# A seven-product matrix kernel on one core: two weight sums queued at the front, and one more stage split a third time

## The chip, the cores and the metric

The kernel runs on one core of one Trainium2 chip. The metric is the device time of an execution in microseconds (us), from the host's view of the device; a profiled execution also has a span, from its first to its last instruction. A core has TensorE (PE, matrix products into PSUM banks), VectorE (DVE, elementwise work), ScalarE (ACT), GpSimd (POOL) and SyncE (SP); in this kernel the last two only start transfers, apart from a small mask at the beginning. Every engine works through its own instructions in order and waits on semaphores of the others.

## The reference

A mixture of eight experts with soft routing: softmax over the experts for each token, and the weighted sum of the experts' matrix products.

```
x (16, 512, 512)   router_logits (16, 512, 8)   expert_weights (8, 512, 2048)
probs = softmax(router_logits)
output = sum over e of probs[:, :, e:e+1] * matmul(x, expert_weights[e])    # (16, 512, 2048) float32
```

## The kernel before

**One large product.** With Z = the tokens' x, scaled by each expert's probability and laid side by side (8192 x 4096), the output is Z times all weights stacked (4096 x 2048). Operands are f16, sums f32. The left operand is made on VectorE, by `times`: x transposed (`xT`) times the probabilities broadcast over partitions (`pT`).

**Three levels of seven products.** A 2 x 2 block product can be made of seven products in place of eight, at the price of sums on both sides (Strassen's way). The kernel does it on three levels.

- Outer level: P1 to P7, on halves of the tokens (pairs of 256 rows, `2q` and `2q + 1`, q from 0 to 15), of the experts and of the columns. `right[r]` holds P_r's weights, `Left` its left operand, `Product` one P_r of one q: 256 rows, depth 2048, 1024 columns.
- Inner level: each of those is seven inner products, run in the order `STEPS = (1, 5, 6, 2, 7, 3, 4)`. Each is 8 matmuls of 128 x 512. Weights 5, 6, 7 and 4 are sums of the four raw blocks, made by `inner_sums` on VectorE: four subtractions over 128 x 4096 (tile `w`). Sum 6 needs sum 5, sum 4 needs sum 6, and sum 7 is written over the block that sum 5 reads. On the left, `queue_s2` makes `d` (for inner product 6) and `queue_i` makes `i` (a `z` made of `z` and `d`, for inner products 7 and 3).
- Third level, in some stages: inner products 1 and 5 of a stage's two products are split into seven again, `by_thirds`: 14 small products of 4 matmuls over 256 columns in place of 4 whole ones. `Thirds.make` makes four left sums for it (128 x 1024), `third_sums` the weights; two of the seven results are added by VectorE in 128 x 256 pieces, on each of the two columns.

**Stages and slots.** A stage is two products, and its inner products alternate: 14 slots, the first product in even slots, the second in odd ones. `run` goes through the stages: P1 in stages 0 to 6 (`ND` = 7 is the first stage of P2), then P2, then P5 and P6, then stage `k7`, which holds P6's last product (6,15) in even slots and P7's first (7,0) in odd ones, then 15 stages of P4 and P7, then P3. A stage by thirds has its inner products 1 and 5 in slots 0 to 3. Before the change, stages 1 to 5 of P1 are by thirds, and stage 6, its last pair, is not. In stage `k7`, inner product 7 of (7,0) is slot 9, and its inner product 4 slot 13.

**What sets VectorE's order.** The program order of VectorE and ScalarE is fixed as the program is written. A planner keeps two clocks, of PE and of VectorE, by costs written in the code (`SLOT` 1.73 for an inner product, 2.29 for a weight sum, 1.22 for a left operand). Work for VectorE is put into `queue` by `later` (at its end, or in front with `first=True`); after each inner product, `slack` takes tasks from the front while VectorE's clock is behind PE's by more than `LAG`. `need` takes all tasks up to one that PE's next step uses, and `flush` is what it uses for that. Evacuations of banks (`post`) are not queued: they are written out where they fall. Hooks put in by `at(stage, slot, ...)` run before the slot's inner product: `sums_at` queues weight sums in this way. After a stage's first slot, `queue_lefts` queues all left operands of the next stage.

P7's four sums are queued by the `sums_at` of line 1086: 5 and 6 in stage `k7 - 1`, 7 in slot 3 of stage `k7`, 4 in its slot 7. P2's are queued in stage 6 (lines 957 to 960).

Of the kernel before, what the change touches and what calls it, by code (L numbers as in the profile page):

```python
# [31 lines left out]
def kernel(  # L32
# [73 lines left out]
    def tt(o, a, b, op):  # L106
        dve(nc.vector.tensor_tensor(out=o, in0=a, in1=b, op=op))  # L107
# [15 lines left out]
    def bank():  # L123
        return psum.tile([P, NB], f32, name="ps", tag="ps")

    def bank2():
        return psum.tile([P, NB], f32, name="pt", tag="pt", bufs=2)
# [6 lines left out]
    def new_w():  # L134
        return wpool.tile([P, K8, NB], f16, name="w", tag="w")

    def new_u():
        return zpool.tile([P, K8, HQ], f16, name="u", tag="u", bufs=1)

    def new_z():  # L140
        return zpool.tile([P, K8, HQ], f16, name="z", tag="z")
# [25 lines left out]
    def inner_sums(b, t7=None):  # L167

        w = {1: b[0, 0], 2: b[1, 0], 3: b[1, 1], 7: t7 or b[0, 1]}

        def step(p, x, y):
            if p not in w:
                w[p] = new_w()
            tt(w[p], x, y, SUB)
        return w, {5: lambda: step(5, b[0, 1], b[0, 0]), 6: lambda: step(6, b[1, 1], w[5]),
                   4: lambda: step(4, b[1, 0], w[6]), 7: lambda: step(7, b[1, 1], b[0, 1])}
# [145 lines left out]
    for n in range(2):  # L322
        ps = [bank2() if n == 0 and j < 2 else bank() for j in range(4)]
        for e in range(HE):
# [4 lines left out]
            if n == 0 and e == 2:  # L329
# [3 lines left out]
                w, sums = inner_sums(b11, new_w())  # L333
# [36 lines left out]
    def flush(task):  # L370
        while task is not None and not task.done:
            queue.popleft().run()

    def need(task):
        if task is not None and not task.done:
            flush(task)
            clock["pe"] = max(clock["pe"], clock["dve"])

    def later(cost, make, first=False):
        t = Task(cost, make)  # L380
        (queue.appendleft if first else queue.append)(t)
        return t
# [58 lines left out]
    def times(z, k, xb, pb):  # L441
        tt(z.rearrange("p (e c) t -> p e c t", e=2), xb.t.unsqueeze(1).to_broadcast([P, 2, C, HQ]),
           pb.t[:, ds(2 * k, 2)].unsqueeze(2).to_broadcast([P, 2, C, HQ]), MUL)

    class Left:
# [6 lines left out]
        def make(self, k):  # L452
            if self.of is not None:
                need(self.of.task[k])
            t = self.t[k] = new_z()
            times(t, k, self.xb, self.pb)
            if self.less is not None:
                u = new_u()
                times(u, k, *self.less)
                tt(t, t, u, SUB)  # L460
            if self.of is not None:
                tt(t, self.of.t[k], t, SUB)
            if self.kept is not None:
                tt(t, t, self.kept.t[:, ds(k * K8, K8), :], SUB)
# [80 lines left out]
    class Right:  # L545
# [6 lines left out]
            self.w, sums = inner_sums(b)  # L552
            return sums

        def queue_sum(self, sums, p):
            self.task[p] = later(2.29, sums[p])

        def op(self, p):
            need(self.task.get(p))
# [65 lines left out]
    ND = 7  # L625
# [28 lines left out]
    def at(stage, slot, make):  # L654
        hooks.setdefault((stage, slot), []).append(make)

    def add(*products):
        stages.append(products)
        return len(stages) - 1


    right = {r: Right() for r in (2, 5, 6, 7, 4, 3)}
# [33 lines left out]
    def product(r, q, **how):  # L696
        left, loads = left_of(r, q)
        lefts[r, q] = left
        p = None
        if r == 1:  # L700
            def sink(tn, o):
                pool(kept_rows(q)(tn), o)
            p = Product(right[1], left, sink)
        elif r == 2:
            if q >= ON_BASE:
                bases[2, q] = Base(kept_rows(q))
            p = Product(right[2], left, to_out(q, 0, 0), bases.get((2, q)))
        elif r == 5:
            bases[6, q] = m1 = Base(kept_rows(q))
            m1.task = {}  # L710

            p = Product(right[5], left, to_out(q, 1, 0))
        elif r == 6:
            m1 = bases[6, q]

            def base(tn):
                need(m1.task[tn])
                return m1.t[tn]
            p = Product(right[6], left, to_out(q, 0, 1), base)
        elif r == 7:  # L720
            base = bases[7, q] = Base(lambda tn: out_rows(q, 0, 1, tn))
            p = Product(right[7], left, to_out(q, 1, 1), base)
        elif r == 4:
            p = Product(right[4], left, to_out(q, 1, 0, accum_op=ADD), products[7, q].o.__getitem__)
        else:
            p = Product(right[3], left, to_out(q, 0, 1, accum_op=ADD), **how)
        p.loads = loads
        products[r, q] = p
        return p
# [137 lines left out]
    k7 = add(some, product(7, 0))  # L867
# [74 lines left out]
    b21, t2 = {}, {}  # L942
# [4 lines left out]
    for kn, where in zip(((0, 0), (0, 1), (1, 1), (1, 0)), ((1, 8), (3, 2), (5, 0), (5, 9))):  # L947
        at(*where, lambda kn=kn: cast21(kn))

    def sums_at(stage, slot, r, of, ps):  # L950
        def go():
            if right[r].w is None:
                right[r].sums = right[r].build(of)
            for p in ps:
                right[r].queue_sum(right[r].sums, p)
        at(stage, slot, go)
    sums_at(ND - 1, 3, 2, b21, (5,))
    sums_at(ND - 1, 5, 2, b21, (6,))
    sums_at(ND - 1, 7, 2, b21, (7,))
    sums_at(ND - 1, 12, 2, b21, (4,))  # L960
    ODD = 0, 1
    for i, (kn, e) in enumerate((kn, e) for kn in (ODD, (0, 0), (1, 1), (1, 0)) for e in range(2)):
        stage = ND + i - 2 if kn != ODD else 2 + 2 * i
        wedge_at(stage, 2, kn, e, (stage + 1, 0))

    def fetch_at_w(stage, slot, of, what, kn):
        at(stage, slot, lambda: of.__setitem__(kn, fetch_w(what, kn)))
# [101 lines left out]
    def turnover(stage, place, r, raw, every=3):  # L1069

        right[r].w = {}

        def fetch(p):
            if p in RAW:
                right[r].w[p] = fetch_w(raw, RAW[p])
            else:
                right[r].w[p] = fetch_w((r, p), (0, 0))
        if every == 3:
            at(stage - 1, 9, lambda: fetch(1))
        for i, p in enumerate(STEPS[every == 3:]):  # L1080
            at(*slots_after(stage, place + 1, every * i), lambda p=p: fetch(p))
    t3 = {}
    for slot, kn in zip((0, 2, 4, 6), ORDER):
        fetch_at_w(k7 - 1, slot, t3, "t3", kn)
    for stage, slot, p in ((k7 - 1, 10, 5), (k7 - 1, 13, 6), (k7, 3, 7), (k7, 7, 4)):
        sums_at(stage, slot, 7, t3, (p,))
    turnover(k7, 0, 4, "t4")
    turnover(k3 - 1, 1, 3, "b22", 2)

# [68 lines left out]
            post(p)  # L1158
    finish.step, finish.post = step_at_end, post_at_end

    for stage in range(1, ND - 1):
        thirds[stage] = Thirds(*(p.left for p in stages[stage]), third)
    for stage in range(ND + 1, last2):
        thirds[stage] = Thirds(*(p.left for p in stages[stage]), third2)
# [44 lines left out]
```

## Time and profile before

| | |
|---|---|
| median of 3 runs | 1374.52 us (1374.25 to 1374.65) |
| profiled execution | 1374.57 us |
| its span | 1372.5 us |
| mean granted clock of TensorE | 0.996 |
| VectorE busy | 1130.7 us, 82% of the span |
| ScalarE busy | 258.8 us, 19% |

How to read it: "PE" rows are matmuls; they are pipelined, so the duration of one (379 ns) is longer than the step from one to the next. "PEld" is the loading of the left operand, which overlaps. All elementwise instructions of VectorE have line 107, that of the helper `tt`, and all matmuls line 130, so they are told apart by tiles: `w` a weight block, `z` a left operand, `d` the left operand of inner product 6, `u` a part of a left operand of two pairs, `xT` and `pT` what it is made of, `ps` and `pt` PSUM banks, `h` results and other half-size tiles. In a timeline, a bracket behind a row gives the idle time before it and what ended it. A group of windows has, for each, its length and the busy time of PE, PEld, DVE, ACT and POOL with the number of instructions, then the granted clock, the share of the DMA engines and GB/s.

### The profile page before, as it was taken

Reading aid. Unit: us, or ns where it says so; the run is one execution under the profiler, and the core shown is the slowest. Engines: PE = TensorE matmul, PEld = TensorE weight load, DVE = VectorE, ACT = ScalarE, POOL = GpSimd, SP = SyncE. Lnnn points to the kernel's source line nnn. Section 1 sums busy time; section 2 is a strip of 40 time slices with the busy share of each in tenths; the row PEclk is TensorE's granted clock in tenths of the full one; section 3 lists DMA queues with packets and bytes.
Section 4 is the critical chain, followed back from the end, with each engine's and each line's share of the span. In section 5 each row is a group of like instructions: output and inputs, shape, how many; then the busy total and the mean of one; then the engine's idle time right before and its main releaser. Section 6 shows DMA issues by size and latency. Waiting matters only on the chain.

```text
span 1372.5 us, 18682 instructions
## 1 busy us (share of the span) xinstructions
PE 1355.9 (99%) x6822; PEld 665.0 (48%) x6822; DVE 1130.7 (82%) x1365; ACT 258.8 (19%) x517; POOL 435.8 (32%) x667
## 2 busy tenths in 40 slices
PE   9999999999999999999999889999999999999998
PEld 4555545565544444444444334444444444556554
DVE  7876677878899888887878987888989888898884
ACT  3233313242211111111111100000000000233331
POOL 3223323332222323223221113344443434233341
PEclk9999999999999999999999989999999999999999
DMA  9999979898999999999987977999999999999997
GB/s 183 245 218 266 246 222 227 256 243 248 255 333 290 281 311 288 281 262 298 299 265 266 345 257 192 229 255 264 255 265 234 270 259 308 336 304 247 207 159 136
DMA packets 190683, 353.55 MB, mean 258 GB/s; under 512 B 52992, under 2 KB 81920, under 8 KB 185856
## 3 DMA queue, kind: packets, MB, share of 16 engines
q0 software_dynamic: 89824, 189.31, 59.1%
q1 hardware_dynamic: 97456, 139.86, 33.8%
q10 hardware_dynamic: 3312, 23.20, 4.4%
q8 instruction: 53, 0.87, 0.3%
q14 instruction: 38, 0.31, 0.1%
HBM read 208.44 MB, written 180.55 MB: 283 GB/s over the span
## 4 chain that ended last, share of the span: by engine, by line
PE 98%; DVE 1%; DMA 0%; issue 0%; POOL 0%; ACT 0%; DVEq 0%; POOLq 0%
PE ps L130 74%; PE pt L130 24%; DVE z L107 1%; DMA w<-in_x_dram 0%; DVE h L107 0%; DVE u L107 0%; DVE w L107 0%; DVE d L107 0%; DVE z L255 0%; POOL w L121 0%; ACT h L1155 0%; DVE lg L295 0%; DVEq L107 0%; POOLq L1193 0%
## 5 line engine op out<-in xcount | busy, mean ns | idle before, releaser
L130 PE MATMUL ps<-w,z 128*128 128x512 f16 (+1 forms) x3768 | 822.1, 375 | 10.9 <-DVE w L107 10.9
L130 PEld LDWEIGHTS <-z 128*128 128x128 f16 x5272 | 516.0, 98 | 590.5 <-issue 13.7
L121 POOL DMA_DIRECT2D out_dram<-h x380 | 256.0, 706 | 698.8 <-ACT h L614 274.2
L130 PE MATMUL pt<-w,z 128*128 128x512 f16 (+1 forms) x1504 | 317.9, 359 | 0.0
L107 DVE TENSOR_TENSOR z<-xT,pT 128x2048 f16<-128x2048 f16 x220 | 265.9, 1216 | 3.5 <-PE pt L130 2.6
L107 DVE TENSOR_TENSOR h<-ps,h 128x512 f32<-128x512 f32 x248 | 168.9, 687 | 95.4 <-PE ps L130 75.3
L130 PE MATMUL ps<-w,d 128*128 128x512 f16 x880 | 199.1, 379 | 0.0
L601 ACT COPY h<-ps 128x512 f32<-128x512 f32 x118 | 69.2, 586 | 420.2 <-PE ps L130 394.3
L130 PEld LDWEIGHTS <-d 128*128 128x128 f16 x880 | 86.0, 98 | 100.1
L107 DVE TENSOR_TENSOR z<-z,d 128x2048 f16<-128x2048 f16 x110 | 131.8, 1216 | 0.0
L107 DVE TENSOR_TENSOR h<-pt,h 128x512 f32<-128x512 f32 x125 | 85.2, 687 | 50.9 <-PE pt L130 49.2
L107 DVE TENSOR_TENSOR w<-w 128x1024 f16<-128x1024 f16 (+2 forms) x105 | 112.3, 1086 | 1.9 <-PE ps L130 1.0
L614 ACT COPY h<-ps 128x512 f32<-128x512 f32 x50 | 29.3, 586 | 402.5 <-PE ps L130 364.6
L107 DVE TENSOR_TENSOR d<-z 128x1024 f16<-128x1024 f16 x110 | 74.6, 684 | 4.5 <-PE ps L130 3.4
L107 DVE TENSOR_TENSOR ps<-ps,h 128x512 f32<-128x512 f32 (+1 forms) x88 | 51.0, 582 | 26.7 <-PE ps L130 23.3
L597 ACT COPY h<-ps 128x512 f32<-128x512 f32 x95 | 52.6, 605 | 70.7 <-PE ps L130 70.7
L121 POOL DMA_DIRECT2D kept<-h x56 | 30.7, 548 | 93.9 <-ACT h L601 53.8
L121 POOL DMA_DIRECT2D out_dram<-kept x56 | 56.4, 1042 | 12.2 <-DMA out_dram<-h 6.3
L593 ACT COPY ps<-ps 128x512 f32<-128x512 f32 x59 | 33.6, 570 | 121.0 <-PE ps L130 65.3
L107 DVE TENSOR_TENSOR ps<-pt,h 128x256 f32<-128x256 f32 x36 | 15.5, 432 | 38.7 <-PE pt L130 26.6
L107 DVE TENSOR_TENSOR h<-h 128x512 f32<-128x512 f32 (+2 forms) x69 | 45.1, 675 | 1.1 <-DMA h<-kept 0.9
L107 DVE TENSOR_TENSOR z<-z,u 128x2048 f16<-128x2048 f16 x36 | 44.1, 1225 | 1.2
(73 smaller groups left out, 543.9 us busy)
## 6 DMA issues: line engine op xcount, KB each, us to landing
out_dram<-h POOLq DMA_DIRECT2D x380, 256.0 KB, 7.3
pT<-p_dram SPq DMA_DIRECT2D x126, 256.0 KB, 7.2
w<-wd ACTq DMA_DIRECT2D x22, 1024.0 KB, 9.5
xT<-x SPq DMA_DIRECT2D x80, 256.0 KB, 7.5
h<-kept SPq DMA_DIRECT2D x72, 256.0 KB, 8.2
h<-out_dram SPq DMA_DIRECT2D x68, 256.0 KB, 6.0
w<-in_expert_weights_dram POOLq DMA_DIRECT2D x33, 512.0 KB, 10.2
kept<-h POOLq DMA_DIRECT2D x56, 256.0 KB, 5.2
```

Of the source, the lines that this page charges most:

```text
L107: dve(nc.vector.tensor_tensor(out=o, in0=a, in1=b, op=op))
L121: note(nc.gpsimd.dma_start(out=o, in_=i, **how))
L130: note(nc.tensor.matmul(ps, z, w, start=start, stop=stop, skip_group_check=True))
L593: act(nc.scalar.copy(self.banks["b"], x))
L597: act(nc.scalar.copy(o[tn], q if p == 5 else x))
L601: act(nc.scalar.copy(o[TN[p]], b if p == 2 else x))
L614: act(nc.scalar.copy(o[tn], b))
```

## The change

P7's sums 7 and 4 are queued one slot later than before (slots 4 and 8 of stage `k7`), but at the front of the queue. As a sum at the front can come ahead of a sum that it depends on, `queue_sum` takes that one first. Stage 6, P1's last, is run by thirds as well, and three of P2's four sums, which are queued in stage 6, are queued two slots later each.

```diff
-        def queue_sum(self, sums, p):
-            self.task[p] = later(2.29, sums[p])
+        def queue_sum(self, sums, p, first=False):
+            def make():
+                flush(self.task.get({6: 5, 7: 5, 4: 6}.get(p)))
+                sums[p]()
+            self.task[p] = later(2.29, make, first)
...
-    def sums_at(stage, slot, r, of, ps):
+    def sums_at(stage, slot, r, of, ps, first=False):
...
-                right[r].queue_sum(right[r].sums, p)
+                right[r].queue_sum(right[r].sums, p, first)
...
-    sums_at(ND - 1, 3, 2, b21, (5,))
-    sums_at(ND - 1, 5, 2, b21, (6,))
-    sums_at(ND - 1, 7, 2, b21, (7,))
+    sums_at(ND - 1, 5, 2, b21, (5,))
+    sums_at(ND - 1, 7, 2, b21, (6,))
+    sums_at(ND - 1, 9, 2, b21, (7,))
...
-    for stage, slot, p in ((k7 - 1, 10, 5), (k7 - 1, 13, 6), (k7, 3, 7), (k7, 7, 4)):
-        sums_at(stage, slot, 7, t3, (p,))
+    for stage, slot, p in ((k7 - 1, 10, 5), (k7 - 1, 13, 6), (k7, 4, 7), (k7, 8, 4)):
+        sums_at(stage, slot, 7, t3, (p,), p in (7, 4))
...
-    for stage in range(1, ND - 1):
+    for stage in range(1, ND):
         thirds[stage] = Thirds(*(p.left for p in stages[stage]), third)
```

## The prediction

> **What bounds the kernel now.** I read the page first. One engine sets the time, TensorE (PE): 1355.9 us busy in a span of 1372.5. The run that was profiled took 1374.57 us, 2.07 more than its span, and the median of the runs before is 1374.52; I make the sum against 1374.57 and leave the 0.05 alone.
>
> ```profile
> span 1372.5 us, 18682 instructions
> PE 1355.9 (99%) x6822; PEld 665.0 (48%) x6822; DVE 1130.7 (82%) x1365; ACT 258.8 (19%) x517; POOL 435.8 (32%) x667
> ```
>
> Time can therefore come off in two ways: fewer matmul columns, or less PE idle time. The second view is the list of waits for PE alone, and it has one entry of weight.
>
> ```profile
> PE ps L130 <- DVE w L107: 10.9, 1, 10.9
> PE every L89 <- DVE h L86: 1.3, 1, 1.3
> ```
>
> One wait of 10.9 us on a weight sum (tile `w`) made by VectorE (DVE). Third view: the timeline of PE around it. Columns are start, duration, engine, line, operation, tiles, count.
>
> ```profile
> 775.74 3.62 PE L130 MATMUL ps<-w,d 128*128 128x512 f16 x16
> 779.20 5.34 PE L130 MATMUL ps<-w,z 128*128 128x512 f16 x24
> 795.46 3.57 PE L130 MATMUL ps<-w,z 128*128 128x512 f16 x8 [10.92 <-DVE w L107]
> 798.82 3.79 PE L130 MATMUL pt<-w,z 128*128 128x512 f16 x16
> 802.46 3.83 PE L130 MATMUL ps<-w,z 128*128 128x512 f16 x17
> ```
>
> An inner product is 8 matmuls and takes one slot. 775.74 to 779.20 is 16 matmuls, so a slot is 1.73 us. The `d` operands mark inner product 6, slots 4 and 5 of a stage; this is stage k7, where P6's last product (6,15) and P7's first (7,0) alternate. Slots 6, 7 and 8 run from 779.20, so slot 8 starts at 782.65 and slot 9 could start at 784.38. It is inner product 7 of (7,0), it needs P7's weight sum 7, and it starts at 795.46: 11.08 us late (the view counts 10.92, from the end of the last matmul). What does DVE do meanwhile? Its timeline:
>
> ```profile
> 774.08 2.28 DVE L107 TENSOR_TENSOR w<-w 128x4096 f16<-128x4096 f16 x1
> 776.27 1.28 DVE L107 TENSOR_TENSOR h<-pt,h 128x512 f32<-128x512 f32 x2
> 777.67 0.69 DVE L107 TENSOR_TENSOR h<-ps,h 128x512 f32<-128x512 f32 x1
> 778.28 0.68 DVE L107 TENSOR_TENSOR h<-h 128x512 f32<-128x512 f32 x1
> 778.88 1.22 DVE L107 TENSOR_TENSOR z<-z,d 128x2048 f16<-128x2048 f16 x1
> 780.01 0.68 DVE L107 TENSOR_TENSOR h<-ps,h 128x512 f32<-128x512 f32 x1
> 780.61 1.22 DVE L107 TENSOR_TENSOR z<-z,d 128x2048 f16<-128x2048 f16 x1
> 781.75 1.22 DVE L107 TENSOR_TENSOR z<-xT,pT 128x2048 f16<-128x2048 f16 x1
> ...
> 784.74 0.68 DVE L107 TENSOR_TENSOR h<-ps,h 128x512 f32<-128x512 f32 x1
> ...
> 789.60 1.22 DVE L107 TENSOR_TENSOR z<-xT,pT 128x2048 f16<-128x2048 f16 x1
> ...
> 793.12 4.49 DVE L107 TENSOR_TENSOR w<-w 128x4096 f16<-128x4096 f16 x2
> 799.07 0.69 DVE L107 TENSOR_TENSOR h<-ps,h 128x512 f32<-128x512 f32 x1 [1.46 <-PE ps L130]
> ```
>
> DVE is never idle from 774.08 to 797.6. The two sums that PE needs in slots 9 and 13 stand last, at 793.12, behind the left operands of the *next* stage (781.75 to 793.12). So this is an order problem: work that is due later stands first. After it PE waits for nothing, while DVE waits 1.46 us for PE at 799.07.
>
> The wait has a second price. Windows of the clock (the column behind POOL is the granted clock):
>
> ```profile
> 787.50:788.50 1.00, 0.00 (x0) 0.00 (x0) 0.97 (x2) 0.00 (x0) 0.00 (x0) 1.00 0.99 397
> 788.50:789.50 1.00, 0.00 (x0) 0.00 (x0) 0.97 (x2) 0.00 (x0) 0.00 (x0) 0.72 1.04 412
> 797.40:798.40 1.00, 1.00 (x4) 0.30 (x3) 0.21 (x1) 0.00 (x0) 0.00 (x0) 0.50 1.01 422
> 798.40:799.40 1.00, 1.00 (x4) 0.40 (x3) 0.33 (x1) 0.00 (x0) 0.00 (x0) 0.61 1.00 420
> ```
>
> At 0.72 the second window spent (0.72 - 0.50)/0.50 = 0.44 us at full clock: the clock halves at 788.94, 4.4 us after PE stopped at 784.54. By the last window it is back at 799.18, 3.7 us after PE resumed. From 795.46 to 802.46 PE did 24 matmuls in 7.00 us, where three slots take 5.18: 1.82 us lost.
>
> **Part 1: the two sums go to the front.** In the built program, VectorE's order from the row at 777.67 on becomes: evacuation of 6.6 (inner product 6 of (6,15)), *sum 7*, evacuation of 7.6, `h<-h`, first `z<-z,d` (operand i of (6,15)), *sum 4*, evacuation of 6.7, second `z<-z,d` (operand i of (7,0)), then the next stage's operands among later evacuations. Nothing is added; two instructions of 4096 columns pass nine or more others. Both are wanted by PE in this stage, but so are the two `z<-z,d`, in slots 8 and 9, and those are now later. I walk it through on the clock of before. Steps from start to start: a sum 2.21 (4.49 for two, less the last one's 2.28), an `h` 0.60 (780.01 to 780.61), a `z` 1.13 (778.88 to 780.01), its result 1.22 after its start, and some 0.04 to reach PE. An evacuation can start 0.36 after its slot (784.74 against 784.38).
>
> - Sum 7: 778.28 to 780.49. PE wants it at 784.38; it is 3.9 us early and this wait is gone.
> - Evacuation of 7.6 to 781.09, `h<-h` to 781.69.
> - i of (6,15): starts 781.69, ready 782.95. Slot 8 wants it at 782.65: **a new wait of 0.30**. Slot 8 ends at 784.68.
> - Sum 4: 782.82 to 785.03. It is wanted only in slot 13, and it stands ahead of i of (7,0).
> - Evacuation of 6.7: can start 784.68 + 0.36 = 785.04, to 785.64.
> - i of (7,0): starts 785.64, ready 786.90. Slot 9 could have started at 784.68: **a new wait of 2.22**.
>
> Slot 9 starts at 786.90 in place of 795.46. New waits together are 2.52 us, against 11.08. The price of these waits is bounded by 0 below (DVE done in time) and 11.08 above (the whole backlog still ahead); I take 2.52 because each of its steps has its own row.
>
> With 0.30 and 2.22 us, both under the 4.4 that passed before the clock halved, I take the 1.82 as saved too. [...]
>
> What is late next: DVE enters stage k7+1 with a backlog, where it was idle in before. Going on with the same steps: PE begins that stage at 786.90 + 5 x 1.73 = 795.5. The first left operand of (7,1) (a `z`, `u`, `z` group takes 3.52: 789.60 to 793.12) is ready at 794.9 and wanted in slot 1, at 797.3. The evacuation of 7.1 by 7.1's own base, which PE's slot 5 has to wait for (same bank), ends at 803.0; slot 5 starts at 804.2. That is the tightest place, with 1.1 us to spare. Later stages have room:
>
> ```profile
> 802.60:826.00 23.40, 23.40 (x111) 10.56 (x109) 20.43 (x24) 1.17 (x2) 4.49 (x7) 1.00 0.64 204
> ```
>
> DVE is busy 20.43 of 23.40 us here, so the debt of a few us is worked off in a stage or two. POOL's and SP's queues keep their order; their transfers only come some 10 us earlier against PE.
>
> **Part 2: stage 6 by thirds.** Stages 1 to 5 already do it, stage 6 does not. The chain of waits dates both:
>
> ```profile
> 140.87 17.27 PE ps L130 x80
> 164.25 20.72 PE ps L130 x96
> 184.97 3.45 PE pt L130 x16
> 209.14 3.45 PE pt L130 x16
> ```
>
> From 140.87 to 164.25 is one stage by thirds, 23.38 us; from 184.97 to 209.14, inner products 5 of stages 6 and 7, is one whole stage, 24.17. **PE gains 0.79 us**: 56 matmuls of 256 columns for 32 of 512. DVE gets four sums of operands and four small additions, dated in stage 4:
>
> ```profile
> 138.36 0.87 DVE L107 TENSOR_TENSOR ps<-pt,h 128x256 f32<-128x256 f32 x2 [2.51 <-PE pt L130]
> 143.19 0.69 DVE L107 TENSOR_TENSOR h<-z 128x1024 f16<-128x1024 f16 x1
> 182.00:206.10 24.10, 24.10 (x113) 10.97 (x112) 17.47 (x15) 5.77 (x11) 4.32 (x8) 1.00 0.53 164
> 191.93 6.81 DVE L107 TENSOR_TENSOR w<-w 128x4096 f16<-128x4096 f16 x3
> 202.95 2.28 DVE L107 TENSOR_TENSOR w<-w 128x4096 f16<-128x4096 f16 x1
> ```
>
> That is 4 x 0.69 + 4 x 0.43 = 4.5 us. Stage 6 has DVE busy 17.47 of 24.10, so 22.0 of the new 23.3: it fits, and I price it at nothing. Three of P2's weight sums are also queued two slots (3.5 us) later. Moved by both, 8 us, sum 5 ends near 202 in place of 194, and stage 7 wants it at 209.14 - 0.79; the last sum, from 202.95, is wanted in slot 12 of stage 7, after 225. If that cover were gone, each us of lateness would be a us of the end. The two buffers of split weights are held four slots longer; sum 5 takes one at slot 5, just after they come free, which is a cost of nothing here.
>
> **Sum.** 1374.57 - (11.08 - 2.52) - 1.82 - 0.79 = **1363.4 us**.
>
> **Rivals.**
> - *The wait grows and the clock falls after all.* If slot 9's wait reaches about 4.4 us (2.2 more; a late load of a base that holds up the evacuation of 6.7 would do it), the 1.82 comes back: 1363.4 + 2.2 + 1.8 = 1367.4. For it: DVE runs in order and sum 4 stands ahead of i of (7,0). Against: nothing waited on a load between 774.08 and 793.12.
> - *The wait only changes its name.* If the backlog ahead of the second `z<-z,d` were as long as that ahead of the sums, PE would lose all 11.08 on `z`: 1374.57 - 0.79 = 1373.8. Against: that backlog consists of the next stage's operands, which stand behind it in the built order.
> - *Slower: the debt is never repaid.* After the wait of before, DVE starts stage k7+1 idle; now it starts behind, and there are 15 stages of P4 and P7. If PE waits at slot 5 of each (bank not yet evacuated), it costs more than the 11.17 won from 0.75 us a stage on; at 1.0 us it is 1363.4 + 15 = 1378.4. Against: 3 us of idle DVE in 802.60:826.00. For: DVE's order over the next three stages is also changed, as the planner now believes PE elsewhere, and an evacuation placed early holds up what stands behind it.
> - *No wait at all*, the lower bound: 1374.57 - 11.08 - 1.82 - 0.79 = 1360.9.
>
> **How the numbers follow.** Forecast, with small misses of a us, 0.80; clock falls 0.07; no wait 0.05; renamed wait 0.05; debt 0.03. The range 1361.0 to 1366.5 reaches from the lower bound to the forecast plus 1.1 (slot 5's margin used up) and 1.8 (clock), and leaves out less than 2 in 10. About 0.2%, 2.75 us, is what a measurement of this kernel can tell: faster is below 1371.8, which holds all but the last two cases, 0.92; the renamed wait is within it, 0.05; the debt is slower, 0.03.
>
> **What would show it.** PE's waits: the entry on `w` of 10.9 gone, one on `z` of about 2.2 and one of 0.3 near 782 to 786 (0.8 earlier, as stage 6 is shorter). The granted clock at 1.00 through that stretch. Stage 6 in 23.4 us with no wait behind it. I am wrong if PE waits on `z`, `d` or `ps` again in stages k7+1 to k7+3, if the clock window shows 0.50, or if stage 7 waits on `w`.

## The result, and the profile after

The changed kernel takes 1368.69 us in the median of six runs (1366.74 to 1371.29), the kernel before 1374.95 on the same chip (1374.25 to 1377.48). The ratio is 0.9953, with a 95% interval of 0.9943 to 0.9963: faster by 0.5%, but by 6.3 us where 11.2 were forecast, and above the range of 1361.0 to 1366.5. The execution that was profiled is one of the faster ones: 1366.88 us, 7.7 below before's 1374.57.

PE's waits in the changed kernel:

```profile
PE ps L130 <- DVE ps L107: 2.8, 1, 2.8
PE ps L130 <- DVE z L107: 2.0, 1, 2.0
PE every L89 <- DVE h L86: 1.3, 1, 1.3
PE ps L130 <- DMA h<-out_dram: 0.8, 1, 0.8
```

The 10.9 us on `w` is gone. The 2.0 on `z` was forecast. The 2.8 and the 0.8 were not. PE's timeline has all three, and gives the price of each step:

```profile
774.61 3.62 PE L130 MATMUL ps<-w,d 128*128 128x512 f16 x16
778.06 5.66 PE L130 MATMUL ps<-w,z 128*128 128x512 f16 x24
785.75 1.90 PE L130 MATMUL ps<-w,z 128*128 128x512 f16 x8 [2.04 <-DVE z L107]
...
790.95 7.07 PE L130 MATMUL ps<-w,z 128*128 128x512 f16 x32
...
802.30 1.89 PE L130 MATMUL ps<-w,d 128*128 128x512 f16 x8 [0.83 <-DMA h<-out_dram]
807.03 1.89 PE L130 MATMUL ps<-w,d 128*128 128x512 f16 x8 [2.84 <-DVE ps L107]
```

Read against before. Slot 4 of stage k7 starts at 774.61 in place of 775.74: 1.13 earlier, stage 6's gain of 0.79 and a start of the kernel that was 0.34 quicker (the same step of stage 5 comes at 140.53 in place of 140.87). Slot 9 starts at 785.75 in place of 795.46: 9.71 earlier, so 8.58 by this stage (8.56 in the forecast). Slot 12 starts at 790.95 in place of 802.46: 11.51 earlier, the further 1.80 being the clock that did not halve (granted 1.00 here, mean of the span 1.000; 1.82 lost before). Up to here everything went as worked out. Then 3.67 us are given back in slots 4 and 5 of stage k7+1, which leaves 7.8; the measured end is 7.7 earlier.

What holds slot 4? VectorE's timeline of the changed kernel from sum 4 on:

```profile
781.68 2.29 DVE L107 TENSOR_TENSOR w<-w 128x4096 f16<-128x4096 f16 x1
...
788.30 1.22 DVE L107 TENSOR_TENSOR z<-xT,pT 128x2048 f16<-128x2048 f16 x1
...
794.16 0.68 DVE L107 TENSOR_TENSOR h<-ps,h 128x512 f32<-128x512 f32 x1
800.95 0.69 DVE L107 TENSOR_TENSOR h<-ps,h 128x512 f32<-128x512 f32 x1 [6.10 <-DMA h<-out_dram]
801.55 0.69 DVE L107 TENSOR_TENSOR ps<-ps,h 128x512 f32<-128x512 f32 x1
...
806.28 0.69 DVE L107 TENSOR_TENSOR ps<-ps,h 128x512 f32<-128x512 f32 x1
```

VectorE, the engine said to be in debt, sits idle for 6.10 us. It is at the evacuation of 7.4 of (7,0), which adds a base from DRAM, and that load has not landed. Slot 4 starts at 802.30, when the row behind it has ended (801.55 + 0.69 = 802.24). The z, u, z group and the evacuation of 7.1 (806.28) stand behind that, so slot 5 waits as well. Where was the load? SyncE's queue, first before the change, then after (start, duration, transfers started):

```profile
772.28 1.44 SPq L118 DMA_DIRECT2D xT<-x  x1
784.85 0.32 SPq L118 DMA_DIRECT2D pT<-p_dram  x1
785.26 3.32 SPq L118 DMA_DIRECT2D h<-out_dram  x4
```

```profile
770.43 2.43 SPq L118 DMA_DIRECT2D xT<-x  x1
789.54 0.32 SPq L118 DMA_DIRECT2D pT<-p_dram  x1
789.96 2.00 SPq L118 DMA_DIRECT2D h<-out_dram  x4
```

The load is the first of the four `h`. Ahead of it stands the load of a `pT` for stage k7+2, which needs a buffer. The buffer comes free when VectorE has made the second `z` of (4,0): at 788.30 + 1.22 = 789.52 after the change, and 789.54 is when the queue goes on; before it, 783.61 + 1.22 = 784.83, and 784.85. The change moved that `z` 4.7 us later by putting two sums ahead of it, and with it, through SyncE's order, a load that has nothing to do with it. VectorE before the change, that `z` and the evacuation of 7.4:

```profile
783.61 1.22 DVE L107 TENSOR_TENSOR z<-xT,pT 128x2048 f16<-128x2048 f16 x1
...
806.11 0.69 DVE L107 TENSOR_TENSOR h<-ps,h 128x512 f32<-128x512 f32 x1 [1.03 <-PE ps L130]
```

Before, the load was used 20.9 us after its issue; now VectorE is ready for it at 794.84, 4.9 us after. It also took longer: 10.9 us from issue to landing, where the same load took 6.9 before. All four base loads did (median in us, first before, then after):

```profile
h<-out_dram SPq DMA_DIRECT2D x4, 256.0 KB, 6.4
```

```profile
h<-out_dram SPq DMA_DIRECT2D x4, 256.0 KB, 11.6
```

The DMA engines are full in that stretch, but so they were before (the last but one column is their share; first before, then after):

```profile
785.00:790.00 5.00, 0.00 (x0) 0.00 (x0) 4.93 (x6) 0.00 (x0) 0.54 (x1) 0.89 0.99 363
```

```profile
790.00:795.00 5.00, 5.00 (x25) 2.25 (x23) 4.81 (x6) 0.00 (x0) 1.00 (x2) 1.00 1.01 404
795.00:801.00 6.00, 6.00 (x29) 2.74 (x28) 0.05 (x1) 0.00 (x0) 0.62 (x2) 1.00 1.02 364
```

So the load was late by 4.7 us through its issue and by about 4 through its landing. An estimate from these rows: had it landed in 6.9 us, VectorE would have gone on at 796.9 in place of 800.95, and the evacuation of 7.1 would have ended at 802.9 in place of 806.97, before slot 5 could have started (802.30 - 0.83 + 1.73 = 803.20). The later issue alone would have cost PE next to nothing. Why the landing was slower stays open: GpSimd started four stores of results between 788 and 796, where before the change it started none between 785.72 and 800.05, but no run separates their effect.

### The profile page after: what moved, and what is told of

Read it like the earlier page. It is cut to its first block, busy times and chain, and to the rows that moved or that the text cites. A ratio compares the mean times of both kernels' runs of the same rounds, so it can differ in the third digit from the quotient of the medians.

```text
span 1365.0 us, 18752 instructions
## 1 busy us (share of the span) xinstructions
PE 1353.4 (99%) x6846; PEld 666.9 (49%) x6846; DVE 1133.9 (83%) x1373; ACT 261.4 (19%) x525; POOL 435.8 (32%) x667
## 4 chain that ended last, share of the span: by engine, by line
PE 97%; DMA 1%; DVE 1%; issue 0%; POOL 0%; ACT 0%; SPq 0%; DVEq 0%; POOLq 0%
PE ps L130 74%; PE pt L130 23%; DMA h<-out_dram 1%; DMA w<-in_x_dram 0%; DVE z L107 0%; DVE w L107 0%; DVE h L107 0%; DVE ps L107 0%; DVE u L107 0%; DVE z L255 0%; POOL w L121 0%; DVE d L107 0%; ACT h L1158 0%; SPq L118 0%; DVEq L107 0%
## 5 line engine op out<-in xcount | busy, mean ns | idle before, releaser
L130 PE MATMUL pt<-w,z 128*128 128x512 f16 (+1 forms) x1488 | 312.7, 357 | 0.0
```

Source lines behind the costliest of these rows:

```text
L130: note(nc.tensor.matmul(ps, z, w, start=start, stop=stop, skip_group_check=True))
```

## The experiments

The theory is the late base load, held in SyncE's queue; its rivals stand with each run.

**The parts one by one.** *Part 1 alone* leaves out the diff's last change and the move of P2's sums; *part 2 alone* restores the queueing of P7's sums.

```diff
# part 1 alone
-    for stage in range(1, ND):
+    for stage in range(1, ND - 1):
# part 2 alone
-    for stage, slot, p in (..., (k7, 4, 7), (k7, 8, 4)):
-        sums_at(stage, slot, 7, t3, (p,), p in (7, 4))
+    for stage, slot, p in (..., (k7, 3, 7), (k7, 7, 4)):
+        sums_at(stage, slot, 7, t3, (p,))
```

> The two sums go to the front, stage 6 stays whole. Theory (the late base load: SyncE holds the load of (7,0)'s base (1,0) behind a pT load that waits for a left operand of the next stage): the same waits as in the changed kernel, about 2.0 us on z in slot 9 of stage k7 and, where the load lands some 11 us after its issue, about 0.8 and 2.8 us in slots 4 and 5 of the next stage; a profiled execution about 0.8 us above the changed kernel's 1366.88, so near 1367.7, and a ratio to before of 0.995 to 0.996. Rival (the two parts disturb each other: the shorter stage 6 shifts transfers and thereby makes the later wait): no wait in slots 4 and 5 of stage k7+1, and about 1364.

> Stage 6 is run by thirds, P7's sums stay at the end of the queue. Theory: 0.79 us of TensorE less and no new wait, so about 1373.8 and the one wait of 10.9 us on w in stage k7 as before. Rival (the four sums and the later weight sums of P2 make stage 7 wait on w, or the split weights hold buffers that a weight transfer needs): a wait near 205 to 225 us and a time at or above before's.

Part 1 alone: 1369.96 us (1368.01 to 1372.75), ratio 0.9963 (0.9949 to 0.9976). Its profiled execution took 1370.73, more than expected, and PE's timeline says why:

```profile
787.05 1.90 PE L130 MATMUL ps<-w,z 128*128 128x512 f16 x8 [2.03 <-DVE z L107]
...
804.21 1.89 PE L130 MATMUL ps<-w,d 128*128 128x512 f16 x8 [1.44 <-DVE ps L107]
808.94 2.40 PE L130 MATMUL ps<-w,d 128*128 128x512 f16 x8 [2.84 <-DVE ps L107]
811.14 8.28 PE L130 MATMUL ps<-w,z 128*128 128x512 f16 x32
```

The same three waits, so they belong to part 1, and the rival (the parts disturb each other) falls. In addition the 32 matmuls from 811.14 take 8.28 us where 7.07 is usual: after the 2.84 the matmuls run slower (the mean granted clock of this execution is 0.999, the changed kernel's 1.000). That cost 1.7 us, and slot 4 waited 0.6 longer than in the changed kernel: together 2.3 of the 3.0 us above the expected 1367.7.

Part 2 alone: 1374.57 us (1373.38 to 1375.11, ten runs) beside 1375.25 before the change, ratio 0.9994 (0.9985 to 1.0002). That is the size expected, and too small for the interval to exclude none. The trace is sharper. The chain of waits of this run:

```profile
164.71 17.27 PE ps L130 x80
188.09 20.72 PE ps L130 x96
208.81 3.45 PE pt L130 x16
```

Stage 6 takes 188.09 - 164.71 = 23.38 us, PE waits for nothing between 100 and 300 us, and the one wait on a weight sum is the 10.9 us in stage k7, as before.

**Moving the load.** *Early base* issues that one load in slot 0 in place of 3, ahead of the stage's operand loads. *Late loads* leaves it and issues the operand loads after slot 3.

```diff
# early base
-            fetch_at(k7 + q - 1 + slot // 14, slot % 14, bases[7, q], tn)
+            fetch_at(k7 + q - 1 + slot // 14, 0 if q == 0 and slot == 17 else slot % 14, bases[7, q], tn)
# late loads
+    late[k7] = 4
```

> The changed kernel, but the load of (7,0)'s base (1,0) is issued in slot 0 of stage k7 in place of slot 3, so that on SyncE's queue it stands ahead of the operand loads of stage k7+2. Theory (late base load): VectorE's idle time of 6.1 us before the evacuation of 7.4 goes, and with it TensorE's waits of 0.8 and 2.8 us in slots 4 and 5 of stage k7+1; about 1363.2 us (1366.88 less 3.67), and less spread between runs than the changed kernel's 1366.7 to 1371.3. Rival (VectorE's own backlog: the z, u, z group ahead of the evacuation of 7.1 is late anyway): a wait of 2 to 3 us in slot 5 of stage k7+1 remains, and the time is 1366 to 1369.

> The changed kernel with the base load left in slot 3 of stage k7; instead the operand loads of stage k7+2, which stood ahead of it on SyncE's queue, are issued after slot 3 (late[k7] = 4). Theory (the queue's order holds the load): the same as with the early base, waits of TensorE in slots 4 and 5 of stage k7+1 gone, 1363.3 to 1365.1 us. Rival (it was the three slots of earlier issue that helped): the waits of 0.8 to 2.1 and 2.8 us stay, 1366.7 to 1372.

Early base: 1364.05 us (1363.30 to 1365.06), ratio 0.9919 (0.9906 to 0.9932). Late loads: 1364.06 (1363.69 to 1365.03), ratio 0.9922 (0.9909 to 0.9936). Both waits are gone in both. Early base, PE's timeline:

```profile
786.40 3.54 PE L130 MATMUL ps<-w,z 128*128 128x512 f16 x8 [2.03 <-DVE z L107]
789.74 3.71 PE L130 MATMUL pt<-w,z 128*128 128x512 f16 x16
793.28 7.07 PE L130 MATMUL ps<-w,z 128*128 128x512 f16 x32
...
803.64 3.62 PE L130 MATMUL ps<-w,d 128*128 128x512 f16 x16
```

Slots 4 and 5 (from 803.64) follow without a gap. Since the load's own place in the code makes no difference once the operand loads stand behind it, it is SyncE's order that held it. (Both runs issue the load 18 to 19 us sooner, so they do not part the later issue from the slower landing.) VectorE's debt as such (the rival) cost nothing in these slots. Yet 786.40 to 793.28 is 6.88 us for 24 matmuls in place of 5.18: in this execution the clock halved after a wait of 2.03 us (granted 0.51 from 786.40 to 789.80), at a price of 1.7. Without it, 1365.06 would be about 1363.4.

**The changed kernel again**, for its spread.

> The changed kernel itself, for its spread on the same chip as the run with the early base. Theory (late base load): the time is about 1363.2 plus what the load's landing costs, which differs from run to run: 1366 to 1371, with the profile showing VectorE idle until a load into h in stage k7+1, by as much longer as the run is slower. Rival (the spread is in the transfers of the whole kernel): before and the run with the early base spread as widely as this one.

1368.15 us (1366.75 to 1372.09, six runs), ratio 0.9950 (0.9937 to 0.9963). The profile is of a run of 1371.37. VectorE's timeline, and PE's:

```profile
803.83 0.69 DVE L107 TENSOR_TENSOR h<-ps,h 128x512 f32<-128x512 f32 x1 [7.36 <-DMA h<-out_dram]
```

```profile
805.18 1.89 PE L130 MATMUL ps<-w,d 128*128 128x512 f16 x8 [2.08 <-DVE ps L107]
809.90 3.11 PE L130 MATMUL ps<-w,d 128*128 128x512 f16 x8 [2.84 <-DVE ps L107]
812.80 7.58 PE L130 MATMUL ps<-w,z 128*128 128x512 f16 x32
```

The load is later by 1.3 us (7.36 for 6.10) and slot 4 waits as much longer (2.08 for 0.83). After the second wait the matmuls run slower (mean granted clock 0.999): 809.90 to 812.80 is 8 matmuls in 2.90 us, not 1.73, and the next 32 take 0.5 more. These two make 2.9 of the 4.5 us between this run and the one of 1366.88; the other 1.6 came before slot 4 of stage k7 (776.24 in place of 774.61). So the theory explains the larger part of the difference between these two executions, and not all; the other runs have no trace. The four runs of the early base lie within 1.8 us, these six within 5.3. But before itself spread from 1374.00 to 1377.91 in 17 runs on this chip, for which I have no cause.

**The remaining wait of 2.0 us.** On top of the early base, operand i of (7,0) is made ahead of sum 4:

```diff
+    at(k7, 8, lambda: flush(stages[k7][1].left.task['i']))
```

> The early base, and operand i of (7,0) is made in slot 8 of stage k7, ahead of sum 4. Theory (the remaining wait of 2.0 us in slot 9 is sum 4's place alone): that wait goes and nothing takes its place, 1364.05 - 2.0 = about 1362. Rival (VectorE owes this work anyway, about 2 us more than its time allows in this stage): the wait in slot 9 goes, and one of 2 to 3 us comes in the first slots of stage k7+1, on a left operand z of (7,1); 1363.5 to 1366.

1366.11 us (1365.91 to 1366.44), ratio 0.9936 (0.9921 to 0.9951): slower than the early base, and than late loads on the same chip (1364.06). PE's timeline:

```profile
782.61 3.63 PE L130 MATMUL ps<-w,z 128*128 128x512 f16 x16 [0.87 <-DVE z L107]
...
797.46 2.63 PE L130 MATMUL ps<-w,z 128*128 128x512 f16 x8 [2.59 <-DVE z L107]
```

Slots 8 and 9 (from 782.61) now follow each other, after a wait of 0.87; the larger wait stands at 797.46, slot 1 of stage k7+1, on the first left operand of (7,1), as the rival said, and a little above its times. The matmuls ran slower after it too (the 8 from 797.46 took 2.42 us to the next start, for 1.73; mean granted clock 0.999), and VectorE was idle once more at a base load of (7,1), 2.56 us until 800.56. But was the work owed, or badly placed? VectorE's timeline of the same run:

```profile
784.54 0.69 DVE L107 TENSOR_TENSOR h<-ps,h 128x512 f32<-128x512 f32 x1 [0.86 <-PE ps L130]
791.45 0.69 DVE L107 TENSOR_TENSOR h<-ps,h 128x512 f32<-128x512 f32 x1 [0.43 <-PE ps L130]
```

VectorE waits for PE at evacuations, 1.3 us in all, while left operands that need nothing from PE stand behind them. Two runs let the planner work ahead in stage k7, also on top of the early base:

```diff
-                slack()
+                slack(lag=-2 if stage == k7 else LAG)      # second run: -3.5
```

> The early base, and in stage k7 the planner takes queued work while VectorE's clock is up to 2 us ahead of TensorE's (in the changed kernel it stops 0.3 us behind). So left operands move ahead of evacuations for which VectorE would sit idle. Theory (part of the owed work fits into VectorE's idle time of this stage): TensorE's wait of 2.0 us on z in slot 9 shrinks or goes, 1361.5 to 1363.5. Rival (no such time is left in that stage, or evacuations that come later hold a bank): a wait on ps takes its place and the time stays at 1364 or above.

> As the run with 2 us, with 3.5. Theory: as there, 1361.5 to 1363.5, and more room in stage k7+1. Rival: evacuations are now late, their results leave later for the buffers h that base loads need, and waits on loads into h appear in the stages after; 1364 to 1368.

With 2 us: 1365.67 (1364.88 to 1367.09), ratio 0.9935 (0.9923 to 0.9948). With 3.5: 1363.32 (1362.86 to 1363.71), ratio 0.9916 (0.9902 to 0.9929). In both the wait in slot 9 is gone, and another has come. Run with 2 us, VectorE's timeline, then PE's:

```profile
795.33 0.69 DVE L107 TENSOR_TENSOR ps<-ps,h 128x512 f32<-128x512 f32 x1
803.37 0.70 DVE L107 TENSOR_TENSOR ps<-ps,h 128x512 f32<-128x512 f32 x1 [7.34 <-DMA h<-out_dram]
```

```profile
805.31 3.51 PE L130 MATMUL ps<-w,d 128*128 128x512 f16 x8 [3.60 <-DVE d L107]
```

Once more VectorE is idle at a base load; now it is the first base of (7,1), the next in the same queue behind the same `pT`. The expectation did not have that; the wait is on `d`, not `ps`, since `d` stands behind that addition. With 3.5 us VectorE is idle for 2.56 us at the same load and for 2.29 until a store out of `h` has ended, and PE waits 1.90 on `z` in slot 7 of stage k7+1. That is near its rival (late results that hold buffers), though the time is the theory's.

**All of it together.** *All bases first* issues the operand loads after slot 7, behind that load too, so that two base loads stand ahead of them; the last run works ahead as well, in two stages. Both start from the changed kernel.

```diff
+    late[k7] = 8
# the second run also
-                slack()
+                slack(lag=-3.5 if stage in (k7, k7 + 1) else LAG)
```

> The changed kernel, with the operand loads of stage k7+2 issued after slot 7 of stage k7 (late[k7] = 8), so that two base loads of stage k7 stand ahead of them on SyncE's queue, (7,0)'s and the first of (7,1). Theory (only the one base load of (7,0) was on the path): the same as with that one load ahead, 1363.3 to 1365.1 us, the wait of 2.0 us in slot 9 unchanged. Rival (more of the base loads are on it, or the operands of stage k7+2 now come too late): under 1363, or a wait on z in stage k7+1 or k7+2 and over 1365.5.

> The same, and in stages k7 and k7+1 the planner takes queued work up to 3.5 us ahead of TensorE's clock. Theory (slot 9's wait needs VectorE's idle time, and working ahead paid for itself only as far as the base loads had landed): no wait of TensorE over 0.5 us from stage k7 to k7+2, 1364.05 - 2.0 = 1361 to 1362.5 us. Rival (VectorE owes the work whatever the loads do): a wait of 1 to 3 us on z, d or ps in one of these stages, and 1363 to 1366.

All bases first: 1364.03 (1362.98 to 1365.77), ratio 0.9920 (0.9905 to 0.9935), no better than with one load moved; the wait of 2.04 us in slot 9 is there as expected. With work ahead: **1361.11 us** (1360.99 to 1362.22), ratio 0.9897 (0.9881 to 0.9914). PE's timeline of the latter, from slot 4 of stage k7:

```profile
775.49 3.62 PE L130 MATMUL ps<-w,d 128*128 128x512 f16 x16
778.95 3.62 PE L130 MATMUL ps<-w,z 128*128 128x512 f16 x16
782.85 3.61 PE L130 MATMUL ps<-w,z 128*128 128x512 f16 x16 [0.29 <-DVE h L107]
...
789.76 7.07 PE L130 MATMUL ps<-w,z 128*128 128x512 f16 x32
796.66 3.62 PE L130 MATMUL pt<-w,z 128*128 128x512 f16 x16
```

From stage k7 on, no wait over 0.3 us is left. VectorE did not owe the work: it had the time, but spent it behind evacuations and loads. This version beats both kernels, and sits at the lower bound of the prediction, 1360.9, which was worked out as no wait at all.

## Why the prediction was wrong

- **Part 1's removed wait.** Right: 8.58 us at slot 9, 8.56 forecast; the new waits of 0.30 and 2.22 came as 0.32 (24 matmuls from 778.06 took 5.66 for 5.34) and 2.04.
- **Next stage, the step that failed.** "POOL's and SP's queues keep their order; their transfers only come some 10 us earlier against PE." The order was kept, but not the times: SyncE's queue stopped for a buffer that VectorE frees (`z` done at 789.52, the queue on at 789.54), and the operands I had counted as passed by the sums are what frees it. The four base loads were issued 4.7 us later and landed in 11.6 us (median) in place of 6.4, while PE came 10 us sooner. Slot 5 was rightly named the tightest place, but its margin of 1.1 us was worked out from VectorE's own instructions, with every operand taken as landed: VectorE stood idle for 6.10 us at the evacuation of 7.4, and PE lost 3.67. Moving that load alone gives 1364.05, within 0.7 us of the forecast of 1363.4.
- **The rival of the late load** named the mechanism in the wrong place (the evacuation of 6.7 in stage k7) and dismissed it with "nothing waited on a load between 774.08 and 793.12". That holds for the changed kernel too, up to 794.84. The load that came late is wanted after that stretch, and before the change the wait of 11 us on `w` had given it time.
- **The clock.** The 1.82 was saved in the execution profiled (mean granted clock 1.000), but by luck. That a wait under 4.4 us is safe was wrong: the clock halved after 2.03 us with the early base (granted 0.51), and after 2.84 the matmuls lost 1.7 us in part 1 alone and in the changed kernel's slower run. It did not halve after 2.04 and 2.84 in the run of 1366.88 (granted 1.00). Of the six runs of the result, four have a mean granted clock of 0.997 to 0.999.
- **Part 2.** Right: stage 6 takes 23.38 us, 0.79 less than 24.17, and no wait follows. The kernel's time was 0.7 lower with it alone, less than the interval can tell from none.
- **The other rivals.** The renamed wait and the debt over 15 stages did not come; beyond slot 5 of stage k7+1 PE waits for nothing in the changed kernel.

## What to carry to other kernels

When work moves later on an engine, list what its end releases, buffers too: here SyncE's queue waited for one, and four base loads that had nothing to do with it went out 4.7 us later behind it. A long stall can hide a late load, as the 10.92 us on `w` did here; before counting it as gained, look up when each load that the next stages need was issued, and whether that time still suffices once the consumer comes sooner, also if the load lands late. And a wait that changes its place with each reordering need not be owed work: look whether the engine is idle at that time, behind something that could have stood later.

## What the runs showed of the hardware that I had not expected

The length of a wait did not decide whether the granted clock fell. Before the change it was 0.50 from 788.94, within the wait of 10.92, to 799.18, for 10.24 us. With the early base it halved after a wait of 2.03 us; in the changed kernel it did not after one of 2.04. Windows of these two runs, first the early base:

```profile
783.00:786.40 3.40, 1.37 (x8) 0.40 (x6) 3.40 (x4) 0.00 (x0) 1.08 (x2) 1.00 1.02 403
786.40:789.80 3.40, 3.40 (x9) 1.20 (x10) 1.77 (x2) 0.00 (x0) 0.00 (x0) 0.51 1.02 424
```

```profile
781.10:784.50 3.40, 2.48 (x11) 0.79 (x9) 3.40 (x4) 0.58 (x1) 0.85 (x2) 1.00 1.02 415
784.50:787.90 3.40, 2.15 (x10) 1.00 (x11) 3.23 (x5) 0.00 (x0) 0.54 (x1) 1.00 0.99 408
...
805.00:808.40 3.40, 1.37 (x7) 0.66 (x7) 3.37 (x6) 0.00 (x0) 0.00 (x0) 1.00 0.81 230
808.40:811.80 3.40, 3.40 (x18) 1.51 (x17) 3.40 (x5) 0.59 (x1) 0.23 (x1) 1.00 0.00 0
```

In the first, the whole wait of 2.03 us lies in one window, PE is busy 1.37 of 3.40, and the clock halves (0.51 in the next). In the second, the wait of 2.04 is shared by two windows with 2.48 and 2.15 busy, and the clock stays at 1.00. But it stays there too after the last window but one, which holds 2.03 us of the wait of 2.84 and has PE busy the same 1.37.

By PE's timelines, six runs lost 1.7 us each to slower matmuls after one wait: of 2.03 us with the early base, 2.04 in all bases first, 2.59 with operand i ahead of sum 4, 2.84 in part 1 alone and in the changed kernel's slower run, 3.60 with 2 us of work ahead. None was lost after 2.03 us with late loads, in part 1 alone and in the changed kernel's slower run, nor after 2.04 and 2.84 in the run of 1366.88. What tells the two kinds of wait apart, no run shows.

The other surprise is the landing time of a load of 256 KB. In the changed kernel the median of all 68 loads into `h` from `out_dram` is 6.4 us, and these four took 11.6; before the change the same four took 6.4, with the DMA engines about as full (a share of 0.99 from 785.00 to 790.00, beside 1.00 from 790.00 to 801.00).
